# A masked softmax on one core: eight slots in place of twelve, loops in place of unrolled code, the mask bound inside the minimum, the first tile in halves

## The chip, the cores and the metric

One NeuronCore of a Trainium2 chip. The metric is the device time of the kernel in microseconds, the median of several executions. Profiles are of one execution each; their span is about 2 us shorter than the timed figure.

## The reference

For each of 16 batches, the softmax over the first `length` of 256 columns; the rest of the row is zero. The data are fp32, 33.5 MB in and 33.5 MB out.

```python
batch, heads, seq_q, seq_k = 16, 8, 256, 256
lengths = np.random.randint(seq_k // 2, seq_k, size=batch)
for b in range(batch):
    masked = x[b, :, :, :lengths[b]] - max over the last axis
    result[b, :, :, :lengths[b]] = exp(masked) / sum(exp(masked))
```

## The kernel before

One batch is one tile of 128 partitions x 16 rows x 256 columns (2.1 MB). The kernel takes the minimum with a bound that is hugely negative beyond the length (no maximum is subtracted), lets ScalarE compute the exponential with its row sum, and lets VectorE multiply by the reciprocal. SyncE loads batches 0 to 3 whole; GpSimd loads the other 12, cut to the smallest of some fixed widths that holds the length.

```python
slots = min(12, batch); ahead = min(4, batch)
xt = pool.tile([P, slots, nt, seq_k], F32, name="xt")
...                                     # SyncE: four loads, then the stores in pieces
load(nc.sync, 0, seq_k)
for b in range(1, ahead):
    load(nc.sync, b, seq_k)
for b in range(batch):
    for s in parts(b):
        nc.sync.wait_ge(s_out, 2 * b + (s.stop - 1) // half + 1)
        nc.sync.dma_start(out=out_f[b, :, s, :], in_=xt[:, b % slots, s, :]).then_inc(s_st[b], 16)
...                                     # GpSimd: zero fills, then 12 loads, unrolled
nc.gpsimd.wait_ge(s_v, 1)
for b in range(ahead, slots):
    nc.gpsimd.memset(xt[:, b, :, low:], 0.0).then_inc(s_fill, 1)
nc.gpsimd.wait_ge(s_ld[ahead - 2], 16)
for n in range(ahead, batch):
    if n < slots:
        nc.gpsimd.wait_ge(s_fill, n - ahead + 1)
    else:
        nc.gpsimd.wait_ge(s_st[n - slots], 16 * len(parts(n - slots)))
    pick(length(POOL, n), n, widths + [seq_k])
...                                     # VectorE: the bound of a batch, and the minimum with it
nc.vector.tensor_scalar(out=cap[:, b % 4, :], in0=iota_h, scalar1=len_s[:, b : b + 1],
                        scalar2=-1.0e30, op0=ALU.subtract, op1=ALU.mult)
nc.vector.tensor_tensor(out=t, in0=t, in1=cap[...].to_broadcast(...), op=ALU.min)
```

The softmax here doesn't subtract the row's maximum and nothing guards it: scores larger than these inputs give would overflow.

## Time and profile before

| | before |
|---|---|
| time, median of 3 runs | 157.55 us (157.49 to 157.84) |
| span of the profile | 155.7 us |
| bytes moved | 62.11 MB, 399 GB/s over the span |
| VectorE / ScalarE busy | 121.3 us / 105.2 us |

The prediction shows the lines and reads them. Here is how to read them. In the rows of 40 slices a digit is the busy share of one slice in tenths. A line of a group gives source line, engine, operation, output<-inputs, count, then busy us, mean ns of one, then the idle time just before these instructions and what ended it. q0 is the queue of DMAs that GpSimd issues, q1 that of SyncE's. A line of a wait gives who waited, for what, us in total, how many times, and the longest. A queue's ring is its line of transfers that are issued and not yet moved.

```profile
SPq L119 <- DVE xt L221: 117.0, 29, 15.4
```

```profile
2.83 0.15 DVE L171 CAST len_b<-word 1x16 bf16<-1x16 int32 x1
2.97 11.04 POOL L145 MEMSET xt<- 128x1536 f32 x8 [0.27 <-DVE iota_h L169]
...
8.96 2.29 DVE L194 TENSOR_TENSOR xt<-xt,cap 128x2048 f32<-128x2048 f32 x1 [3.00 <-DMA xt<-in_x_dram]
...
18.59 17.98 SPq L119 DMA_DIRECT2D out_dram<-xt  x9
```

The first mask begins at 8.96 us, the first store is issued at 18.59.

### The profile page before, as it was taken

The page shows a single profiled execution, that of the slowest core. Times are in us where ns is not written, and L with a number is a line of the kernel's source. Part 1 is how long each engine was busy: PE and PEld are TensorE (multiplying, and loading weights), DVE is VectorE, ACT ScalarE, POOL GpSimd, SP SyncE. Part 2 cuts the span into 40 slices and gives each one's busy share as a digit, 9 for nine tenths or more (in the row PEclk, how much of TensorE's full clock was granted, in tenths as well). Part 3 has the DMA queues.
Part 4 walks back from the last instruction along what each step waited for, and adds up shares of the span by engine and source line. Part 5 has one row for each costly group of instructions (what it writes and reads, how often), then busy time and mean ns, then how long its engine had stood idle before and what let it go on. Part 6 is the DMA issues. An engine that isn't in the chain of part 4 may idle for free.

```text
span 155.7 us, 1168 instructions
## 1 busy us (share of the span) xinstructions
PE 0.2 (0%) x1; PEld 0.1 (0%) x1; DVE 121.3 (78%) x99; ACT 105.2 (68%) x514; POOL 25.1 (16%) x27
## 2 busy tenths in 40 slices
PE   0000000000000000000000000000000000000000
PEld 0000000000000000000000000000000000000000
DVE  2567999999999998949995999997977999910000
ACT  3009999997979695957978397979592989400000
POOL 5996045743001102010000000000000000000000
DMA  4999999999999999999999999999999999999990
GB/s 131 417 450 417 434 368 388 412 445 415 390 398 409 413 421 408 426 400 411 415 412 419 403 409 412 408 418 409 422 436 416 423 434 427 442 429 438 406 402 25
DMA packets 10311, 62.11 MB, mean 399 GB/s; under 512 B 914, under 2 KB 1010, under 8 KB 7106
## 3 DMA queue, kind: packets, MB, share of 16 engines
q1 hardware_dynamic: 6192, 41.95, 65.4%
q0 software_dynamic: 4112, 20.12, 32.0%
q14 instruction: 5, 0.04, 0.1%
q10 hardware_dynamic: 2, 0.00, 0.0%
HBM read 28.51 MB, written 33.55 MB: 399 GB/s over the span
## 4 chain that ended last, share of the span: by engine, by line
DVE 33%; DMA 30%; issue 12%; POOL 6%; another core or an unknown queue 4%; POOLq 1%; SPq 1%; DVEq 0%
DMA xt<-in_x_dram 30%; DVE xt L221 18%; DVE xt L194 12%; POOL xt L145 4%; POOL xt L108 2%; DVE inv_sum L219 1%; DVE cap L179 1%; POOLq L100 1%; SPq L108 1%; POOLq L133 0%; DVEq L207 0%; POOLq L135 0%; DVEq L206 0%; SPq L269 0%
## 5 line engine op out<-in xcount | busy, mean ns | idle before, releaser
L237 ACT ACTIVATE xt<-xt x256 | 102.4, 401 | 27.2 <-DVE xt L194 27.2
L221 DVE TENSOR_TENSOR xt<-xt,inv_sum 128x2048 f32<-128x2048 f32 x32 | 73.3, 2292 | 1.1
L237 ACT ACTIVATION_READ_ACCUMULATOR xt<-xt x256 | 47.8, 187 | 0.0
L194 DVE TENSOR_TENSOR xt<-xt,cap 128x2048 f32<-128x2048 f32 x16 | 36.6, 2287 | 11.6 <-DMA xt<-in_x_dram 11.5
L108 POOL DMA_DIRECT2D xt<-in_x_dram x12 | 12.8, 1065 | 41.3 <-issue 41.3
L145 POOL MEMSET xt<- 128x1536 f32 x8 | 11.0, 1427 | 0.3 <-DVE iota_h L169 0.3
L179 DVE TENSOR_SCALAR cap<-iota_h,len_s 128x256 f32<-128x256 f32 x16 | 9.1, 572 | 0.0
L219 DVE RECIPROCAL inv_sum<-row_sum 128x8 f32<-128x8 f32 x32 | 6.3, 195 | 0.0
L169 DVE TENSOR_SCALAR iota_h<-iota_i 128x256 f32<-128x256 int32 x1 | 0.3, 294 | 2.6 <-POOL iota_i L139 2.6
L230 ACT ACT_TABLE_LOAD x1 | 1.3, 1283 | 1.5 <-SPq L81 1.5
L138 POOL DMA_DIRECT2D word_p<-in_lengths_dram x1 | 0.6, 633 | 1.1 <-SPq L81 1.1
L173 DVE COPY len_s<-len_f 128x16 f32<-128x16 f32 x1 | 0.2, 176 | 0.3 <-PE len_f L158 0.3
L139 POOL IOTA iota_i<- 128x256 int32 x1 | 0.4, 360 | 0.1
L230 ACT ACTIVATE warm<-const-float32-0.0 128x1 f32<-128x1 f32 x1 | 0.2, 203 | 0.0
L142 POOL MEMSET ones<- 1x128 bf16 x1 | 0.2, 195 | 0.0
L158 PE MATMUL len_f<-len_b,ones 1*128 1x16 bf16 x1 | 0.2, 167 | 3.1 <-DVE len_b L171 3.1
L171 DVE CAST len_b<-word 1x16 bf16<-1x16 int32 x1 | 0.2, 154 | 0.0
L258 POOL MEMSET const-float32-0.0<- 128x1 f32 x1 | 0.1, 99 | 0.2 <-issue 0.2
L158 PEld LDWEIGHTS len_f<-len_b,ones 1*128 1x128 bf16 x1 | 0.1, 100 | 3.1 <-POOL ones L142 3.1
L258 POOL MEMSET const-float32-1.0<- 128x1 f32 x1 | 0.1, 98 | 0.0
L258 POOL MEMSET const-bfloat16-1.0<- 128x1 bf16 x1 | 0.1, 98 | 0.0
L258 POOL MEMSET const-uint8-127<- 128x1 uint8 x1 | 0.1, 98 | 0.0
## 6 DMA issues: line engine op xcount, KB each, us to landing
out_dram<-xt SPq DMA_DIRECT2D x16, 1024.0 KB, 24.0
out_dram<-xt SPq DMA_DIRECT2D x20, 512.0 KB, 24.3
xt<-in_x_dram SPq DMA_DIRECT2D x4, 2048.0 KB, 14.4
out_dram<-xt SPq DMA_DIRECT2D x3, 2048.0 KB, 19.1
xt<-in_x_dram POOLq DMA_DIRECT2D x3, 1728.0 KB, 54.8
xt<-in_x_dram POOLq DMA_DIRECT2D x2, 2048.0 KB, 38.3
xt<-in_x_dram POOLq DMA_DIRECT2D x2, 1600.0 KB, 36.6
xt<-in_x_dram POOLq DMA_DIRECT2D x2, 1280.0 KB, 62.5
```

The lines of the kernel that those rows point to most:

```text
L100: return nc.values_load((word_p if engine == POOL else word)[0:1, 2 * b : 2 * b + 1], engines=[engine], skip_runtime_bounds_check_because= ...
L108: engine.dma_start(out=xt[:, b % slots, :, :w], in_=x_f[b, :, :, :w]).then_inc(s_ld[b], 16)
L138: nc.gpsimd.dma_start(out=word64_p, in_=lengths[None, :]).then_inc(s_word_p, 16)
L139: nc.gpsimd.iota(iota_i, pattern=[[1, seq_k]], base=0, channel_multiplier=0).then_inc(s_iota, 1)
L145: nc.gpsimd.memset(xt[:, b, :, low:], 0.0).then_inc(s_fill, 1)
L179: nc.vector.tensor_scalar(out=cap[:, b % 4, :], in0=iota_h, scalar1=len_s[:, b : b + 1], scalar2=-1.0e30, op0=ALU.subtract, op1=ALU.mult,)
L194: return nc.vector.tensor_tensor(out=t[:, :, lo:hi], in0=t[:, :, lo:hi], in1=cap[:, b % 4, None, lo:hi].to_broadcast([P, nt, hi - lo]), op ...
L219: step(nc.vector.reciprocal(out=inv_sum[:, b, s], in_=row_sum[:, b, s]))
L221: ins = nc.vector.tensor_tensor(out=t[:, s, :], in0=t[:, s, :], in1=inv_sum[:, b, s, None].to_broadcast([P, half, seq_k]), op=ALU.mult,)
L230: nc.scalar.activation(out=warm, in_=nc.const_aps.tensor(0.0, (P, 1), F32), func=EXP)
L237: ins = nc.scalar.activation(out=e, in_=e, func=EXP, accum_out=row_sum[:, bass.ds(i, 1), j],)
L258: nc = _bacc.Bacc("TRN2", target_bir_lowering=False, num_devices=1)
```

## The change

Its intent: shorter programs and less memory at no loss, some work taken off VectorE, and an earlier first store. The core of the diff, cut:

```diff
-    slots = min(12, batch)
+    slots = 8
-        load(nc.sync, 0, seq_k)
+        for h in range(2):
+            s = slice(h * half, (h + 1) * half)
+            nc.sync.dma_start(out=xt[:, 0, s], in_=x_f[0, :, s]).then_inc(s_ld[h], 16)
 ...
+                if b >= 2 and s.start == 0:
+                    nc.sync.wait_ge(s_b, 64 * (b // 2 + 1))      # store b waits for store b-2
 ...
-        for n in range(ahead, batch):
-            ...
-            pick(length(POOL, n), n, widths + [seq_k])
+        with nc.Fori(0, (batch - ahead) // 2, 1, engines=[POOL]) as q:
+            for par in range(2):
+                n = 2 * q + (ahead + par)
+                v_len = length(POOL, word_p[0:1, bass.ds(2 * n, 1)])
+                with nc.gpsimd.If(q >= 1):
+                    nc.gpsimd.wait_ge(s_sw[par], 16 * q)         # load n-2
+                    nc.gpsimd.wait_ge(s_st[par], 64 * q)         # store n-8
+                pick(v_len, bass.ds(n, 1), bass.ds(n % slots, 1), par, widths + [seq_k])
 ...
-            return nc.vector.tensor_tensor(out=t, in0=t, in1=cap, op=ALU.min)
+            return nc.vector.scalar_tensor_tensor(
+                out=t, in0=down, scalar=len_s[:, b : b + 1], in1=t, op0=ALU.add, op1=ALU.min)
 ...
-        mask(0)                       # then mask(b+1) ahead of both divides of b
+        mask(0, slice(0, half))
+        mask(0, slice(half, nt))      # then divide(0, 0), mask(1), divide(0, 1), ...
 ...
-        for first, last in ((0, slots), (slots, batch)):      # ScalarE: 16 rows a round
+        with nc.Fori(0, 2 * batch, 1, engines=[ACT]) as i:    # ScalarE: 8 rows a round
```

GpSimd's iota now comes ahead of its DMA of the lengths.

More of the change, by code (lines that the diff above doesn't have):

```diff
@@ L14 @@
 EXP = mybir.ActivationFunctionType.Exp
-SP = mybir.EngineType.SP
 DVE = mybir.EngineType.DVE
@@ L36 @@
     half = nt // 2
+    quarter = nt // 4
     x_f = x.rearrange("b h q k -> b (h q) k").rearrange("b (p t) k -> b p t k", p=P)
     out_f = out.rearrange("b h q k -> b (h q) k").rearrange("b (p t) k -> b p t k", p=P)
-    slots = min(12, batch)
-    ahead = min(4, batch)
+    slots = 8
+    ahead = 4
+    assert slots - ahead == 4 and batch % slots == 0
     widths = list(range(160, 248, 8))
     low = widths[0]
-    quarter = nt // 4
-    cuts = lambda b: (
-        [0, half, half + quarter, nt]
-        if b < slots - 2
-        else [0, half, nt]
-        if b < slots or b == batch - 1
-        else [0, nt]
-    )
-    def parts(b):
-        return [slice(i, j) for i, j in zip(cuts(b), cuts(b)[1:])]
-    mid = seq_k // 2
+    mid = seq_k // 2
+    big = 1.0e30
+    def parts(b):
+        if b < 10:
+            cuts = [0, half, half + quarter, nt]
+        elif b < 12 or b == batch - 1:
+            cuts = [0, half, nt]
+        else:
+            cuts = [0, nt]
+        return [slice(i, j) for i, j in zip(cuts, cuts[1:])]
     pool = ctx.enter_context(tc.tile_pool(name="all", bufs=1))
@@ L73 @@
     iota_i = pool.tile([P, seq_k], I32, name="iota_i")
-    iota_h = pool.tile([P, seq_k], F32, name="iota_h")
-    cap = pool.tile([P, 4, seq_k], F32, name="cap")
+    down = pool.tile([P, seq_k], F32, name="down")
     row_sum = pool.tile([P, batch, nt], F32, name="row_sum")
@@ L78 @@
     warm = pool.tile([P, 1], F32, name="warm")
-    sem = lambda n: ctx.enter_context(nc.semaphore(n))
+    seed = pool.tile([1, 2], F32, name="seed")
     with tc.tile_critical(no_gpsimd_drain=True):
+        sem = lambda n: ctx.enter_context(nc.semaphore(n))
         s_word = sem("s_word")
@@ L86 @@
         s_lenf = sem("s_lenf")
-        s_ld = [sem(f"s_ld{b}") for b in range(batch)]
-        early = batch - slots
-        s_st = [sem(f"s_st{b}") for b in range(early)] + [sem("s_st")] * slots
+        s_ld = [sem(f"s_ld{k}") for k in range(ahead + 1)]
+        s_sw = [sem("s_sw0"), sem("s_sw1")]
+        s_st = [sem("s_st0"), sem("s_st1")]
         s_iota = sem("s_iota")
@@ L96, with length @@
         s_out = sem("s_out")
-        def length(engine, b):
+        def length(engine, at):
             return nc.values_load(
-                (word_p if engine == POOL else word)[0:1, 2 * b : 2 * b + 1],
+                at,
                 engines=[engine],
@@ L104, in length, with pick @@
             )
-        def load(engine, b, w):
-            engine.dma_start(
-                out=xt[:, b % slots, :, :w], in_=x_f[b, :, :, :w]
-            ).then_inc(s_ld[b], 16)
-        load(nc.sync, 0, seq_k)
+        for h in range(2):
+            s = slice(h * half, (h + 1) * half)
+            nc.sync.dma_start(out=xt[:, 0, s], in_=x_f[0, :, s]).then_inc(s_ld[h], 16)
         nc.scalar.dma_start(out=word64, in_=lengths[None, :]).then_inc(s_word, 16)
         for b in range(1, ahead):
-            load(nc.sync, b, seq_k)
+            nc.sync.dma_start(out=xt[:, b], in_=x_f[b]).then_inc(s_ld[b + 1], 16)
         for b in range(batch):
+            s_b = s_st[b % 2]
             for s in parts(b):
                 nc.sync.wait_ge(s_out, 2 * b + (s.stop - 1) // half + 1)
+                if b >= 2 and s.start == 0:
+                    nc.sync.wait_ge(s_b, 64 * (b // 2 + 1))
                 nc.sync.dma_start(
                     out=out_f[b, :, s, :], in_=xt[:, b % slots, s, :]
-                ).then_inc(s_st[b], 16)
-        nc.sync.wait_ge(s_st[-1], 16 * sum(len(parts(b)) for b in range(early, batch)))
-        def pick(v, b, ws):
+                ).then_inc(s_b, 16 * ((s.stop - s.start) // quarter))
+        for par in range(2):
+            nc.sync.wait_ge(s_st[par], 64 * (batch // 2 + 1))
+        def pick(v, n, slot, par, ws):
             if len(ws) == 1:
-                load(nc.gpsimd, b, ws[0])
+                w = ws[0]
+                nc.gpsimd.dma_start(
+                    out=xt[:, slot, :, :w], in_=x_n[:, n, :, :w]
+                ).then_inc(s_sw[par], 16)
                 return
@@ L133, in pick @@
             with nc.gpsimd.If(v <= ws[m]):
-                pick(v, b, ws[: m + 1])
+                pick(v, n, slot, par, ws[: m + 1])
             with nc.gpsimd.Else():
-                pick(v, b, ws[m + 1 :])
-        nc.gpsimd.dma_start(out=word64_p, in_=lengths[None, :]).then_inc(s_word_p, 16)
+                pick(v, n, slot, par, ws[m + 1 :])
+        x_n = x_f.rearrange("b p t c -> p b t c")
         nc.gpsimd.iota(
@@ L142 @@
         nc.gpsimd.memset(ones, 1.0).then_inc(s_ones, 1)
+        nc.gpsimd.dma_start(out=word64_p, in_=lengths[None, :]).then_inc(s_word_p, 16)
+        for par in range(2):
+            nc.gpsimd.memset(seed[:, par : par + 1], 0.0).then_inc(s_st[par], 64)
         nc.gpsimd.wait_ge(s_v, 1)
@@ L146 @@
         nc.gpsimd.wait_ge(s_word_p, 16)
-        nc.gpsimd.wait_ge(s_ld[ahead - 2], 16)
-        for n in range(ahead, batch):
-            if n < slots:
-                nc.gpsimd.wait_ge(s_fill, n - ahead + 1)
-            else:
-                nc.gpsimd.wait_ge(s_st[n - slots], 16 * len(parts(n - slots)))
-            pick(length(POOL, n), n, widths + [seq_k])
+        nc.gpsimd.wait_ge(s_fill, slots - ahead)
+        nc.gpsimd.wait_ge(s_ld[ahead - 1], 16)
+        with nc.Fori(0, (batch - ahead) // 2, 1, engines=[POOL]) as q:
+            for par in range(2):
+                n = 2 * q + (ahead + par)
[4 more added lines that the diff above has]
+                pick(v_len, bass.ds(n, 1), bass.ds(n % slots, 1), par, widths + [seq_k])
         nc.tensor.wait_ge(s_ones, 1)
@@ L168 @@
         nc.vector.wait_ge(s_iota, 1)
-        step(nc.vector.tensor_scalar(out=iota_h, in0=iota_i, scalar1=0.5, scalar2=None, op0=ALU.add))
+        step(
+            nc.vector.tensor_scalar(
+                out=down, in0=iota_i, scalar1=0.5, scalar2=-big, op0=ALU.add, op1=ALU.mult
+            )
+        )
         nc.vector.wait_ge(s_word, 16)
@@ L172 @@
         nc.vector.wait_ge(s_lenf, 1)
-        step(nc.vector.tensor_copy(out=len_s, in_=len_f))
-        nc.vector.wait_ge(s_v, v)
-        def make_cap(b):
-            step(
-                nc.vector.tensor_scalar(
-                    out=cap[:, b % 4, :],
-                    in0=iota_h,
-                    scalar1=len_s[:, b : b + 1],
-                    scalar2=-1.0e30,
-                    op0=ALU.subtract,
-                    op1=ALU.mult,
-                )
-            )
-            return v
@@ L190 @@
-        cap_at = {b: make_cap(b) for b in range(2)}
-        def clip(b, lo, hi):
-            t = xt[:, b % slots]
-            return nc.vector.tensor_tensor(
-                out=t[:, :, lo:hi],
-                in0=t[:, :, lo:hi],
-                in1=cap[:, b % 4, None, lo:hi].to_broadcast([P, nt, hi - lo]),
-                op=ALU.min,
-            )
-        def mask(b):
-            if b + 1 < batch and b + 1 not in cap_at:
-                cap_at[b + 1] = make_cap(b + 1)
-            v_len = length(DVE, b)
-            nc.vector.wait_ge(s_v, cap_at[b])
-            nc.vector.wait_ge(s_ld[b], 16)
-            with nc.vector.If(v_len < mid):
-                clip(b, 0, mid)
-            clip(b, mid, seq_k).then_inc(s_min, 1)
@@ L211 @@
-        mask(0)
-        for b in range(batch):
-            if b + 1 < batch:
-                mask(b + 1)
-            t = xt[:, b % slots]
-            for h in range(2):
-                s = slice(h * half, (h + 1) * half)
-                nc.vector.wait_ge(s_exp, 2 * b + h + 1)
-                step(nc.vector.reciprocal(out=inv_sum[:, b, s], in_=row_sum[:, b, s]))
-                nc.vector.wait_ge(s_v, v)
-                ins = nc.vector.tensor_tensor(
-                    out=t[:, s, :],
-                    in0=t[:, s, :],
-                    in1=inv_sum[:, b, s, None].to_broadcast([P, half, seq_k]),
-                    op=ALU.mult,
-                )
-                ins.then_inc(s_out, 1)
@@ L230 @@
-        nc.scalar.activation(out=warm, in_=nc.const_aps.tensor(0.0, (P, 1), F32), func=EXP)
-        for first, last in ((0, slots), (slots, batch)):
-            with nc.Fori(first, last, 1, engines=[ACT]) as i:
-                nc.scalar.wait_ge(s_min, i + 1)
-                slot = i - first
-                for j in range(nt):
-                    e = xt[:, bass.ds(slot, 1), j, :]
-                    ins = nc.scalar.activation(
-                        out=e,
-                        in_=e,
-                        func=EXP,
-                        accum_out=row_sum[:, bass.ds(i, 1), j],
-                    )
-                    if (j + 1) % half == 0:
-                        ins.then_inc(s_exp, 1)
+        step(
+            nc.vector.tensor_scalar(
+                out=len_s, in0=len_f, scalar1=big, scalar2=None, op0=ALU.mult
+            )
+        )
@@ new lines, with clip, mask @@
+        nc.vector.wait_ge(s_v, v)
+        def clip(b, s, lo, hi):
+            t = xt[:, b % slots, s, lo:hi]
+            return nc.vector.scalar_tensor_tensor(
+                out=t,
+                in0=down[:, None, lo:hi].to_broadcast([P, s.stop - s.start, hi - lo]),
+                scalar=len_s[:, b : b + 1],
+                in1=t,
+                op0=ALU.add,
+                op1=ALU.min,
+            )
+        def mask(b, s):
+            v_len = length(DVE, word[0:1, 2 * b : 2 * b + 1])
+            if b == 0:
+                nc.vector.wait_ge(s_ld[s.start // half], 16)
+            elif b < ahead:
+                nc.vector.wait_ge(s_ld[b + 1], 16)
+            else:
+                nc.vector.wait_ge(s_sw[b % 2], 16 * ((b - ahead) // 2 + 1))
+            with nc.vector.If(v_len < mid):
+                clip(b, s, 0, mid)
+            clip(b, s, mid, seq_k).then_inc(s_min, (s.stop - s.start) // half)
@@ new lines, in divide @@
+        def divide(b, h):
+            s = slice(h * half, (h + 1) * half)
+            nc.vector.wait_ge(s_exp, 2 * b + h + 1)
+            step(nc.vector.reciprocal(out=inv_sum[:, b, s], in_=row_sum[:, b, s]))
+            nc.vector.wait_ge(s_v, v)
+            t = xt[:, b % slots, s, :]
+            nc.vector.tensor_tensor(
+                out=t,
+                in0=t,
+                in1=inv_sum[:, b, s, None].to_broadcast([P, half, seq_k]),
+                op=ALU.mult,
+            ).then_inc(s_out, 1)
@@ new lines @@
+        mask(0, slice(0, half))
+        mask(0, slice(half, nt))
+        for b in range(batch):
+            if b == 0:
+                divide(0, 0)
+            if b + 1 < batch:
+                mask(b + 1, slice(0, nt))
+            if b > 0:
+                divide(b, 0)
+            divide(b, 1)
+        nc.scalar.activation(out=warm, in_=nc.const_aps.tensor(0.0, (P, 1), F32), func=EXP)
+        x_h = xt.rearrange("p s (h j) c -> p (s h) j c", h=2)
+        sum_h = row_sum.rearrange("p b (h j) -> p (b h) j", h=2)
@@ L247 @@
+        with nc.Fori(0, 2 * batch, 1, engines=[ACT]) as i:
+            nc.scalar.wait_ge(s_min, i + 1)
+            at = bass.ds(i % (2 * slots), 1)
+            for j in range(half):
+                e = x_h[:, at, j, :]
+                ins = nc.scalar.activation(
+                    out=e, in_=e, func=EXP, accum_out=sum_h[:, bass.ds(i, 1), j]
+                )
+            ins.then_inc(s_exp, 1)
 _INS = ['x', 'lengths']
```

## The prediction

> **What bounds the kernel now.** I read the page first, for which row is full; then the busy time by stretch, for where it is full; then the queues of one stretch, for what shares the full resource; then the groups and the timelines, for how close the engines come to being the limit themselves.
>
> The page: span, two rows of the 40 slices (each 3.9 us), and the two DMA queues (packets, MB, share of the 16 engines' span).
>
> ```profile
> span 155.7 us, 1168 instructions
> ...
> DVE  2567999999999998949995999997977999910000
> ...
> DMA  4999999999999999999999999999999999999990
> GB/s 131 417 450 417 434 368 388 412 445 415 390 398 409 413 421 408 426 400 411 415 412 419 403 409 412 408 418 409 422 436 416 423 434 427 442 429 438 406 402 25
> ...
> q1 hardware_dynamic: 6192, 41.95, 65.4%
> q0 software_dynamic: 4112, 20.12, 32.0%
> ```
>
> The DMA row is 9 from the second slice to the last but one. VectorE is at 9 too for long stretches, but its row is 0 for the last four slices, while the DMA stays full: what ends the kernel is transfer, not arithmetic. q0 holds the 12 loads that GpSimd issues (cut to a width of 160 to 256 columns by the batch's length); q1 holds the first four loads and every store.
>
> By stretch (columns: PE, PEld, DVE, ACT, POOL busy us, clock, DMA share, GB/s):
>
> ```profile
> 20.00:30.00 10.00, 0.00 (x0) 0.00 (x0) 9.93 (x9) 10.00 (x51) 6.16 (x6) 1.00 0.99 387
> ...
> 60.00:70.00 10.00, 0.00 (x0) 0.00 (x0) 7.89 (x7) 6.58 (x33) 1.02 (x2) 1.00 1.02 414
> ...
> 110.00:120.00 10.00, 0.00 (x0) 0.00 (x0) 8.06 (x7) 6.49 (x32) 0.00 (x0) 1.00 1.03 432
> ...
> 140.00:150.00 10.00, 0.00 (x0) 0.00 (x0) 0.00 (x0) 0.00 (x0) 0.00 (x0) 1.00 0.99 423
> 150.00:156.00 6.00, 0.00 (x0) 0.00 (x0) 0.00 (x0) 0.00 (x0) 0.00 (x0) 1.00 0.30 128
> ```
>
> After 140 us all compute engines show 0.00 and the DMA still moves 423 GB/s: a backlog of stores is drained. The sum of the bytes confirms it: 62.11 MB in all, less 0.52 MB before 4 us (131 GB/s) and 0.77 MB after 150 us (128 GB/s), is 60.8 MB in 146 us, 417 GB/s. So time = about 2.5 us until the stream starts, 62.11 MB at 417 GB/s = 149 us, some 4 us for the last landing and the end of the span, and about 2 us by which the timed run (157.55) exceeds the span (155.7).
>
> The queues in the stretch from 60 to 90 us:
>
> ```profile
> q1 hardware_dynamic: 1388, 6.62, 54.3%
> q0 software_dynamic: 1393, 5.75, 47.8%
> ```
>
> Both always have work, and take turns. The groups (busy us, mean ns of one, idle before):
>
> ```profile
> L237 ACT ACTIVATE xt<-xt x256 | 102.4, 401 | 27.2 <-DVE xt L194 27.2
> L221 DVE TENSOR_TENSOR xt<-xt,inv_sum 128x2048 f32<-128x2048 f32 x32 | 73.3, 2292 | 1.1
> ...
> L194 DVE TENSOR_TENSOR xt<-xt,cap 128x2048 f32<-128x2048 f32 x16 | 36.6, 2287 | 11.6 <-DMA xt<-in_x_dram 11.5
> ...
> L179 DVE TENSOR_SCALAR cap<-iota_h,len_s 128x256 f32<-128x256 f32 x16 | 9.1, 572 | 0.0
> ```
>
> VectorE waits 11.5 us for loads in its masks, ScalarE 27.2 us for VectorE. From the timelines, three instructions of VectorE and the last four loads of GpSimd:
>
> ```profile
> 21.19 2.29 DVE L194 TENSOR_TENSOR xt<-xt,cap 128x2048 f32<-128x2048 f32 x1
> ...
> 28.55 2.27 DVE L194 TENSOR_TENSOR xt<-xt,cap 128x2048 f32<-128x2048 f32 x1
> ...
> 134.71 2.29 DVE L221 TENSOR_TENSOR xt<-xt,inv_sum 128x2048 f32<-128x2048 f32 x1
> ```
>
> ```profile
> 35.47 1.26 POOL L108 DMA_DIRECT2D xt<-in_x_dram x1 [2.37 <-issue]
> 50.01 1.15 POOL L108 DMA_DIRECT2D xt<-in_x_dram x1 [13.28 <-issue]
> 59.31 1.15 POOL L108 DMA_DIRECT2D xt<-in_x_dram x1 [8.15 <-issue]
> 67.50 0.56 POOL L108 DMA_DIRECT2D xt<-in_x_dram x1 [7.04 <-issue]
> ```
>
> VectorE, when never waiting, takes 28.55 - 21.19 = 7.36 us a batch; the DMA takes 149 / 16 = 9.3 us. VectorE's last work ends at 137.0, some 17 us before the transfers: 17 us at 425 GB/s is 7 MB, over three batches of stores. The four loads reuse the slots of batches 0 to 3, so they tell when those stores had landed: about 34, 49, 58 and 66 us, some 10.7 us apart.
>
> [...]
>
> **The change, part by part.**
> (1) Bytes: none. The widths of the 12 loads are picked as before, and the stores are cut as before (ten batches in three pieces, two in two, three whole, the last in two: 39 both times). The sum of 149 us stays.
> (2) Mask: 16 bounds of 572 ns go, 9.1 us busy, but most of that overlaps: in the steady cadence one adds only about 0.27 us, the 20.93 to 21.19 us between its start and that of the mask behind it. The minimum becomes scalar-tensor-tensor over the same 2048 columns. [...] it costs 2.29 us, and VectorE's cadence is 7.36 - 0.27 = 7.1 us against the DMA's 9.3. Gain on the path: none; it was waiting for loads already.
> (3) First tile in halves: its first half should land about 2.4 us sooner (1 MB at 430 GB/s), and the first store can be issued at some 13.5 us: half landed at 6.5 (mask 0 began at 8.96), half a mask 1.15, eight exponentials 8 x 0.4 = 3.2, divide 2.3, latencies. Before it was 18.6. But the store enters the same ring behind loads 1 to 3 (8.4 MB, done at about 21 us at 430 GB/s), so it starts to move at 21 us either way. What is left is a fuller store queue in the stretch 20 to 30 us, which ran at 387 instead of 411 GB/s: at most 10 x 24 / 411 = 0.6 us, and I count half, 0.3 us.
> (4) ScalarE's loop over halves: 32 rounds in place of 16; 256 exponentials at 0.40 us as before, 6.4 us a batch, perhaps 0.3 us for one more loop turn (the idle 0.31 us that one batch's start shows). Under 7.1 us: nothing on the path.
> (5) Eight slots, and at most two loads and two stores in flight: load n now waits for load n-2 and store n-8, store b for store b-2. Loads landed some 8.4 us apart in the later part (mask 8 waited until 68.8, mask 14 until 117.9). When load n-2 lands, load n-1 still has some 8 us in the ring, and GpSimd needs 2 to 3 us for its branches and its 1.15 us issue: q0 does not run dry. Store n-8, from the 10.7 us spacing: store 0 at 34 against load 6 at about 50 (needed for load 8), store 4 at 77 against load 10 at 85, store 7 at 109 against load 13 at 108. The slack shrinks to nothing for the last load, but load 14 then still covers 8 us. When a store lands, the one behind it holds 2.1 MB, 5 us at full rate, longer than a wake-up. So both rings stay fed, and the round robin stays as it was.
> Sum: 157.55 - 0.3 = 157.2 us.
>
> **The rivals.**
> A: the mask at half rate. [...] I give it one chance in five.
> B: the slots or the short queues starve the DMA. For: the slack of about zero at the last load. Against: VectorE's lead at the end is 17 us. Load 15 landed before 125 us; its mask, exponentials and divides took 12 us, and a last half store 4.5. To reach 161 us it would have to land some 17 us later. I expect 0 to 1.5 us.
> C: fewer loads queued give stores a larger share early, or the fuller store queue helps more: all would have to come from 411 GB/s rising towards 432. Over 100 us of mixed traffic that would be 5 us at most; nothing in the change alters packet sizes, so I count on under 1 us.
>
> **Range and chances.** The main line gives 156.5 to 158 us; B adds up to 1.5[...]. Predicted 157.2, range 155.8 to 160.2. Slower by 2% means over 160.7: most of half of A, and a little of B, 0.11. Faster by 2% means under 154.4, which needs C in full: 0.03. Within: 0.86.
>
> **What would show it.** DMA row still at 9 with about 62.1 MB; q0 and q1 packets equal in mid-run, q0 ending at about 121 us; the mask's group at about 2290 ns for the 15 whole tiles; VectorE ending 10 us or more before the span does. The prediction is wrong if [...] DMA slices in the middle fall below 9.

Passages are cut out of the text above, and the cuts are marked: rules and figures that no trace or run of this case shows. They are the paragraph ahead of the parts of the change, with an upper limit on what another order could win; in part (2) the condition for the 2.29 us, that the new mask runs as fast as the minimum it replaces (2287 ns), which no run had shown yet; and the arithmetic of rival A, the reasons for and against it, and two clauses of the last paragraphs that used it. The sum came to 157.55 - 0.3 = 157.2 us, but its zero for the mask rests on that condition. Rival A's came to 159.5 to 162.5 us; it stands in the range's upper end and in the chance of 0.11. The wake-up of part (5), given there without a figure, is short in the trace after: in 14 waits for a store SyncE issued the next one 0.06 to 0.07 us after the landing.

## More of the kernel before

```profile
20.00:24.00 4.00, 0.00 (x0) 0.00 (x0) 3.96 (x5) 4.00 (x21) 1.78 (x3) 1.00 0.97 363
```

Before, every store waits for VectorE alone, and the little cast of the lengths (2.83 us) comes just ahead of GpSimd's fills (2.97 us).

## The result, and the profile after

| | before | after |
|---|---|---|
| time, median of 6 runs each | 157.61 us (157.44 to 157.84) | 157.14 us (156.85 to 157.49) |
| ratio of fast runs | | 0.997 (95%: 0.9954 to 0.9985) |
| span of the profile | 155.7 us | 155.5 us |
| VectorE busy | 121.3 us | 120.0 us |
| GB/s, 20 to 24 us | 363 | 293 |

A ratio is the mean time of one kernel's fast runs over the mean of the other's of the same rounds, so it is not quite the ratio of the medians. Executions over 1.5% slower than the fastest of the same kernel are left out of the means. The change is within 2%, 0.3% faster and just clear of noise.

The page of the kernel after:

```profile
DVE  4963999999999968939895999997977999920000
...
DMA  4999999999999999999999999999999999999991
GB/s 116 428 443 426 434 312 388 416 442 427 393 395 410 415 416 406 420 410 413 409 412 419 402 417 406 415 411 405 425 421 432 420 419 432 457 426 422 415 434 61
...
q1 hardware_dynamic: 6336, 41.95, 65.9%
q0 software_dynamic: 4112, 20.12, 32.0%
```

The bytes of both queues are those of before. The DMA row is full again from the second slice, and VectorE's row again ends in four zeros. (Single slices of the GB/s row reach 450 before and 457 after because the view books all of a packet's bytes at its start. With the bytes spread over each packet's own time, read from the kept traces, every microsecond from 16 to 20 us has 429 to 432 GB/s in both kernels.) The queues of the stretch from 60 to 90 us, after:

```profile
q1 hardware_dynamic: 1381, 6.59, 54.1%
q0 software_dynamic: 1377, 5.76, 47.9%
```

They still take turns one to one, as before. What did move is who waits for what. The waits of SyncE's queue, after:

```profile
SPq L118 <- DMA out_dram<-xt: 98.5, 14, 11.0
```

SyncE used to wait for VectorE for 117.0 us; now 98.5 us are waits for an earlier store. It looks alarming and costs nothing that shows: while SyncE waits for store b-2, store b-1 is in the ring, and the DMA row stays at 9.

The groups of VectorE after, with different shapes kept apart:

```profile
L197 DVE SCALAR_TENSOR_TENSOR xt<-down,len_s,xt 128x2048 f32<-128x2048 f32 x15 | 35.2, 2347 | 10.2 <-DMA xt<-in_x_dram 10.2
...
L185 DVE CAST len_b<-word 1x16 bf16<-1x16 int32 x1 | 5.6, 5595 | 0.4 <-DMA word<-in_lengths_dram 0.4
```

The new mask takes 2347 ns, against 2287 before: 2.6% more, so no half rate. The second line is the surprise: a cast of 16 numbers takes 5.6 us. The timeline of the first 17 us, after, shows why:

```profile
2.30 5.59 DVE L185 CAST len_b<-word 1x16 bf16<-1x16 int32 x1 [0.40 <-DMA word<-in_lengths_dram]
...
2.54 5.33 POOL L151 MEMSET xt<- 128x1536 f32 x4
...
9.29 2.48 DVE L197 SCALAR_TENSOR_TENSOR xt<-down,len_s,xt 128x1024 f32<-128x1024 f32 x2 [0.87 <-DVE len_s L188]
...
16.73 5.82 SPq L119 DMA_DIRECT2D out_dram<-xt  x3
```

The cast ends at 7.89 us, with the last of the fills at 7.87. The fills now come before the cast has run, and the first mask needs the lengths; so the first half tile, landed by about 6.5 us (as the run with the later fills shows), waits until 9.29 us, later than the whole tile of before (8.96). The cast took 5595 ns, where it took 154 ns before. What holds it can't be read from the stamps alone: the cast's record starts 0.24 us ahead of that of the fills, and at its old length it would have been over before them. That it is the fills that hold it is shown by the run with the later fills, below.

### The profile page after: what moved, and what is told of

Read it like the earlier page. It is cut to its first block, busy times and chain, and to the rows that moved or that the text cites. A ratio compares the mean times of both kernels' runs of the same rounds, so it can differ in the third digit from the quotient of the medians.

```text
span 155.5 us, 1320 instructions
## 1 busy us (share of the span) xinstructions
PE 0.2 (0%) x1; PEld 0.1 (0%) x1; DVE 120.0 (77%) x84; ACT 105.1 (68%) x514; POOL 19.4 (12%) x26
## 3 DMA queue, kind: packets, MB, share of 16 engines
q1 hardware_dynamic: 6336, 41.95, 65.9%
## 4 chain that ended last, share of the span: by engine, by line
DMA 67%; DVE 11%; issue 6%; POOLq 2%; SPq 1%; POOL 0%; DVEq 0%
DMA xt<-in_x_dram 60%; DVE xt L224 7%; DMA out_dram<-xt 7%; DVE xt L197 3%; POOLq L100 1%; POOLq L136 1%; POOLq L131 1%; SPq L109 1%; DVE inv_sum L221 0%; POOL xt L131 0%; SPq L112 0%; POOLq L159 0%; POOLq L155 0%; DVEq L214 0%; POOLq L161 0%
## 5 line engine op out<-in xcount | busy, mean ns | idle before, releaser
L251 ACT ACTIVATE xt<-xt x256 | 102.4, 402 | 27.2 <-DVE xt L197 27.2
L197 DVE SCALAR_TENSOR_TENSOR xt<-down,len_s,xt 128x2048 f32<-128x2048 f32 (+1 forms) x17 | 37.7, 2222 | 11.1 <-DMA xt<-in_x_dram 10.2
L185 DVE CAST len_b<-word 1x16 bf16<-1x16 int32 x1 | 5.6, 5595 | 0.4 <-DMA word<-in_lengths_dram 0.4
L151 POOL MEMSET xt<- 128x1536 f32 x4 | 5.3, 1392 | 0.0
```

The lines of the kernel that those rows point to most:

```text
L185: nc.vector.tensor_copy(out=len_b, in_=word[:, ::2]).then_inc(s_lenb, 1)
L197: return nc.vector.scalar_tensor_tensor(out=t, in0=down[:, None, lo:hi].to_broadcast([P, s.stop - s.start, hi - lo]), scalar=len_s[:, b : ...
L251: ins = nc.scalar.activation(out=e, in_=e, func=EXP, accum_out=sum_h[:, bass.ds(i, 1), j])
```

## The experiments

Theory T: the transfers alone set the time, and every part of the change lies off that path. Rivals: a lighter VectorE, fewer queued loads, or the earlier first store made the 0.3%; the mask has little slack; the slots have little slack. Twelve kernels were run.

**The mask alone.** In the kernel before, the bounds go and the minimum becomes the new form.

```diff
-step(make_cap ...)   # 16 bounds
-nc.vector.tensor_tensor(out=t, in0=t, in1=cap, op=ALU.min)
+nc.vector.scalar_tensor_tensor(out=t, in0=iota_h, scalar=len_s[:, b : b + 1], in1=t, op0=ALU.add, op1=ALU.min)
```

> The kernel before with one part alone: the bound is added inside the minimum, the 16 separate bounds are gone. Theory T (transfers set the end, the mask is off the path): 157.3 to 157.9 us, ratio to before within 0.3% of 1, VectorE cadence about 7.1 in place of 7.36 us, mask about 2350 ns, waits of VectorE for loads longer by what it saves. Rival (the 0.3% came from a lighter VectorE): ratio about 0.997, 157.1 us.

Measured: 157.46 us, ratio 0.9987 (0.9973 to 1.0002). Its groups:

```profile
L178 DVE SCALAR_TENSOR_TENSOR xt<-iota_h,len_s,xt 128x2048 f32<-128x2048 f32 x16 | 37.6, 2349 | 17.5 <-DMA xt<-in_x_dram 17.4
```

VectorE's busy time fell from 121.3 to 114.5 us, by 6.8, and its waits for loads rose from 11.5 to 17.4, by 5.9. What VectorE saves here, off the path, it waits.

**Eight slots alone.** In the kernel before, with the pieces of the stores kept.

```diff
-    slots = min(12, batch)
+    slots = min(8, batch)
```

> The kernel before with eight slots in place of twelve and nothing else (same store pieces). Theory T: 157.3 to 158.0 us, q0 and q1 packets still equal from 60 to 90 us, q0 ending at about 121 us. Rival B (slots starve the transfers): DMA slices under 9 in mid-run and a time over 158.5 us. Rival (fewer loads queued gave the 0.3%): ratio about 0.997.

Measured: 157.34 us, ratio 0.9979 (0.9964 to 0.9994), 1387 packets of q1 to 1388 of q0 from 60 to 90 us. No starving; a gain of 0.2% that just clears noise, between theory T and the rival of fewer queued loads. That rival is not excluded for a part of the 0.3%, though fewer slots still do not gain more, as the next run shows.

**Six slots, and five.** The same edit with 6 and with 5.

> The kernel before with six slots, store pieces as they were. At 9.3 us a batch six slots turn round in 56 us. A batch holds its slot for about 16 us of load, 15 to 20 of compute and 20 to 24 of store, together 51 to 60, so loads begin to run dry; but then stores get the whole rate, so the transfers stay full: 157.3 to 159 us. Rival B (short of slots, the transfers starve): over 160.

Measured: 157.64 us, ratio 0.9992 (0.9968 to 1.0015); one of its four runs was slow (160.71 us) and is not counted.

> The kernel before with five slots, one more than the four first loads: 46 us a turn, under the 51 to 60 that a batch holds its slot with both queues full. Theory: now loads and stores must each move faster than with both queues full, holes appear in the DMA row: 158.5 to 163 us. Rival (the split of the rate adapts without holes): within 0.5% of before.

Measured: 159.32 us, ratio 1.0114 (1.0082 to 1.0145). The page with five slots:

```profile
DVE  2264999999919898079699959996971979999900
...
GB/s 121 421 446 417 446 348 413 413 419 430 435 390 409 393 425 409 424 408 408 382 410 416 414 414 413 411 411 415 422 418 414 415 422 434 409 434 181 409 425 167
```

The mid-run that I expected to show holes has none beyond the dip at 20 us (348), which the kernel before has too (368). Even here the split of the rate adapts: from 33.3 to 39.2 us q0 moves no data, and q1 alone fills the engines (419 and 430 GB/s in the two slices from 31.4 to 39.3 us). The hole is at the end, in the slice with 181 GB/s: the last load is issued at 121.9 us (67.5 with twelve slots, 105.4 with eight, 118.1 with six), VectorE works on until 149 us (its row ends in two zeros, not four), and the backlog of stores that used to cover the last batch's arithmetic is used up. So in the kernel before slots run short between six and five, and it shows as a thinner cushion at the end.

**The mask twice.** In the changed kernel each mask is computed once more into a spare tile; the results are the same, and VectorE pays about what a mask at half rate would cost, one more mask of 2347 ns.

```diff
+            step(clip(b, s, mid, seq_k, out=spare[:, s, :]))
+            nc.vector.wait_ge(s_v, v)
             clip(b, s, mid, seq_k).then_inc(s_min, ...)
```

> The changed kernel with each mask computed once more into a spare tile: the same results, VectorE dearer by 16 x some 2.4 us, which is what a mask at half rate would have cost. If VectorE's slack of 17 us at the end is all there is, 38 us more must show: VectorE full from 9 us on, cadence 7.13 + 2.4 = 9.55 us, 9.3 + 2.4 + 16 x 9.55 = 164.5 us, half a store 4.5 behind it: span 167 to 169, time 168 to 171 us, 7 to 8% slower. If transfers alone decide: still 157.

Measured: 174.24 us, ratio 1.1054 (1.1036 to 1.1073). A second mask of a whole tile takes 2.45 us from its start to that of the next (17.95 to 20.40 us, for one). VectorE's row of the page, and the end of the timeline:

```profile
DVE  5887999999999999999999999999999999999910
```

```profile
159.54 5.24 SPq L120 DMA_DIRECT2D out_dram<-xt  x3
...
162.10 2.29 DVE L227 TENSOR_TENSOR xt<-xt,inv_sum 128x2048 f32<-128x2048 f32 x1
```

VectorE is the bound from start to end and finishes at 164.4 us, as expected (164.5). The time is still 3 us over my range, because the tail behind VectorE is 8.0 us (the span is 172.4) and not 4.5. Batch 14 is stored in one piece, so nothing of it can leave before its second half is divided at 159.5; with batch 15 that is 4.2 MB, 9.8 us at 430 GB/s, from 159.5 on. The long pieces cost nothing that shows behind the backlog of the changed kernel (157.14 us, against 157.04 for the transfers alone, below), and cost here, where VectorE is last.

**The fills later.** In the changed kernel the fills wait until the lengths are scaled.

```diff
-        nc.gpsimd.wait_ge(s_v, 1)
+        nc.gpsimd.wait_ge(s_v, 2)
```

> The changed kernel with GpSimd's four fills held back until the lengths have been scaled (a wait for 2 in place of 1). Theory: the cast of the lengths took 5.6 us because it stood behind the fills; it will take about 0.15 us, the first mask begins at about 6.5 us in place of 9.3, the first store is issued at about 14 in place of 16.7. As the store lies behind loads 1 to 3 in its ring, the time changes by under 0.3 us: 156.8 to 157.3. Rival: the early store is worth its full 2.7 us, 154.5.

Measured: 157.27 us, ratio 0.9977 (0.9958 to 0.9995), so no better than the changed kernel's 0.997 of other rounds. Its timeline:

```profile
2.29 0.16 DVE L185 CAST len_b<-word 1x16 bf16<-1x16 int32 x1 [0.39 <-DMA word<-in_lengths_dram]
...
3.04 5.33 POOL L151 MEMSET xt<- 128x1536 f32 x4 [0.45 <-DVE len_s L188]
6.58 1.28 DVE L197 SCALAR_TENSOR_TENSOR xt<-down,len_s,xt 128x1024 f32<-128x1024 f32 x1 [3.60 <-DMA xt<-in_x_dram]
...
14.01 0.42 SPq L119 DMA_DIRECT2D out_dram<-xt  x1
```

The cast is back to 0.16 us, the first mask comes at 6.58 us and the first store at 14.01, all as expected, and the time does not move. Note too that the mask at 6.58 us runs its 1.28 us beside the fills (3.04 to 8.37 us), as long as the second half's at 9.05 us after them, where the cast could not. So the fills were what held the cast, and the early store is worth nothing that these runs can tell, far from the rival's 2.7 us.

**The transfers alone.** In the changed kernel masks, exponentials and divides go, and a store waits for its load (a wrong result).

```diff
-                nc.sync.wait_ge(s_out, 2 * b + (s.stop - 1) // half + 1)
+                nc.sync.wait_ge(s_ld[...] or s_sw[b % 2], ...)     # the load of batch b
-        ... all of mask, divide and ScalarE's loop
```

> The changed kernel with masks, exponentials and divides taken out; every store waits for its load's landing alone (a wrong result on purpose: the inputs come back). The same 62.1 MB in the same pieces on the same queues. Theory T: the transfers alone take nearly as long, 155 to 157.2 us. Rival (waits of stores and loads for the compute engines cost several us): 152 or less.

Measured: 157.04 us, ratio 0.9956 (0.994 to 0.9972). Against the changed kernel's 157.14 (ratio 0.997, of other rounds), all the arithmetic together costs no more than a few tenths of a microsecond; the intervals overlap. This is the plainest proof that the arithmetic is off the path. The run keeps the order of the transfers and the depth of the queues, so it says nothing of these.

**Fewer bytes.** In the changed kernel every load of GpSimd's takes 160 columns. Its output is wrong, which doesn't matter for the time.

```diff
-                w = ws[0]
+                w = low
```

> The changed kernel with every one of GpSimd's 12 loads cut to 160 columns (a wrong result on purpose where a length is over 160), everything else as it was: 536 columns x 2048 rows x 4 B = 4.39 MB fewer. Theory T: the time falls with the bytes, 4.39 MB at 417 GB/s = 10.5 us[...]: 146 to 149 us. Rival (compute or waits set the end): over 154 us.

(A term that no run shows is cut out of this expectation; the range of 146 to 149 us stands as it was written, with that term.)

Measured: 147.16 us, ratio 0.9335 (0.9321 to 0.9348). 4.39 MB fewer, 10.0 us less: 439 GB/s for the marginal byte. T again: the time follows the bytes.

**The hole at 20 us, 1: loads sooner.** Both kernels lose rate from 20 to 24 us, the changed one more (293 GB/s against 363).

```diff
-        nc.gpsimd.wait_ge(s_ld[ahead - 1], 16)
+        nc.gpsimd.wait_ge(s_ld[ahead - 2], 16)
```

> The changed kernel with GpSimd's loads waiting for batch 1 to land and not for batch 2, some 4.8 us sooner. In both kernels the transfers drop from 20 to 24 us (363 GB/s before, 293 after, against 430 ahead of it), as the first four loads are done and load 4, issued at 20.7, has not started to move. Theory: the hole is 0.55 MB, 1.3 us, and closes: load 4 is issued at about 16, the stretch 20 to 24 us runs at over 400 GB/s, 155.7 to 156.5 us. Rival (the hole's bytes are made up later, or load 3 is delayed as much): 156.9 to 157.4.

Measured: 156.78 us, ratio 0.9949 (0.9937 to 0.9961), between the range of the theory and that of the rival. Load 4 was issued at 15.80 us, but the stretch only rose from 293 to 324 GB/s, under a third of what I expected: my reason for the hole was wrong.

**2: both.** Sooner loads and later fills.

> The changed kernel with the fills held back until the lengths are scaled, and the loads sooner as well. The first store is then issued at about 14 us as with the fills alone, load 4 at about 16. Theory: the sum of the two, 155.5 to 156.3 us, the fastest so far; if the first store's place in the ring behind loads 1 to 3 makes it worthless, the same as the sooner loads alone within 0.2 us.

Measured: 156.67 us, ratio 0.9937 (0.9922 to 0.9952), the lowest median of all, but not the sum: it is within 0.2 us of the sooner loads alone, so the later fills add nothing clear. What the sooner loads gain on the changed kernel (0.9949 against 0.997, of other rounds) is at the edge of noise. In the same rounds the transfers alone, in the changed kernel's order, took 157.04: with all its arithmetic this version is no slower.

**3: the first tile in halves alone,** in the kernel before.

```diff
-        load(nc.sync, 0, seq_k)
+        nc.sync.dma_start(out=xt[:, 0, :half], in_=x_f[0, :, :half]).then_inc(s_ld[0], 16)
+        nc.sync.dma_start(out=xt[:, 0, half:], in_=x_f[0, :, half:]).then_inc(s_first, 16)
         # mask 0, its exponentials and divide(0, 0) by halves, ahead of mask 1
```

> The kernel before with one part alone: the first tile is loaded and masked in halves, its first divide comes before mask 1. Here the lengths are cast ahead of the fills, so nothing holds the first mask: it begins at about 6.5 to 7 us, unless the two bounds ahead of it are held up by the fills to a later time (they took 2.4 us in the kernel before, until 5.9). First store at about 14 us in place of 18.6. Theory (the store lies behind loads 1 to 3 in its ring): 157.3 to 157.8 us. Rival (an early store is worth its 4.6 us): 153.

Measured: 158.08 us, ratio 1.0024 (1.0007 to 1.0041): above my range and a little slower than before, just clear of noise, though the first mask came at 6.43 us and the first store at 13.71, just as the prediction had them for the changed kernel.

**4: loads at once,** with no wait for an earlier load, and the later fills.

```diff
-        nc.gpsimd.wait_ge(s_ld[ahead - 1], 16)
```

> The changed kernel with the fills held back and GpSimd's loads waiting for no earlier load at all: load 4 is issued at about 10 us and moves from about 14. What is open: the hole at 20 to 24 us stayed with the loads sooner (322 in place of 293 GB/s) and was there too with no compute at all (262), where stores had been queued since 6.4 us. If it is the start of q0, it moves to about 14 us; if it is the turn of q1 from loads to stores, it stays where q1 turns, somewhat later than 20 us as loads 2 and 3 now share the rate, and is shallower, as q0 is then in full flow. Time 156.0 to 156.7 us.

Measured: 156.95 us, ratio 0.995 (0.9934 to 0.9967), a little above my range.

The rate by stretch shows what the hole goes with (columns as in the prediction, the last is GB/s). The changed kernel, the first tile in halves alone, the transfers alone (its ScalarE is idle and has no column), and the loads at once:

```profile
16.00:20.00 4.00, 0.00 (x0) 0.00 (x0) 3.97 (x4) 2.12 (x12) 0.00 (x0) 1.00 1.01 430
20.00:24.00 4.00, 0.00 (x0) 0.00 (x0) 3.97 (x4) 4.00 (x22) 1.71 (x2) 1.00 0.96 293
```

```profile
20.00:24.00 4.00, 0.00 (x0) 0.00 (x0) 3.93 (x5) 4.00 (x22) 1.69 (x2) 1.00 0.93 287
```

```profile
20.00:24.00 4.00, 0.00 (x0) 0.00 (x0) 0.00 (x0) 1.74 (x2) 1.00 0.93 262
```

```profile
20.00:24.00 4.00, 0.00 (x0) 0.00 (x0) 3.65 (x3) 4.00 (x21) 0.00 (x0) 1.00 1.03 409
24.00:26.00 2.00, 0.00 (x0) 0.00 (x0) 1.97 (x3) 2.00 (x11) 0.00 (x0) 1.00 0.89 269
```

With the transfers alone, stores had been issued behind the loads from 6.4 us on, and the hole is deepest: it is no lack of work. With the loads at once q0 moves from about 15 us, and no hole comes there; it moves to 24 to 26 us, where q1 runs out of loads and turns to stores, as loads 2 and 3 now share the rate. So the hole goes with q1's turn from loads to stores.

Packet by packet, the kept traces say more. In the changed kernel the 16 KB packets of SyncE's last loads that start between 21 and 22 us take 1.14 us in the median, where those from 12 to 20 us take 0.61; the first packet of a store starts only at 23.43. (Before: 0.79 us, and 22.67.) So it is the last packets of the loads that slow down, while stores stand behind them. Why is open.

What makes it deeper is open too. All eight kernels with the first tile in halves that turn near 20 us have 262 to 324 GB/s from 20 to 24 us, all five with a whole first tile 350 to 371. The count of stores that stand ready does not explain it by itself: the mask twice issues its first store at 18.05 us, half a microsecond ahead of the kernel before, and has 311; the later fills issue theirs 2.7 us ahead of the changed kernel and have 299 against 293. These rates are of one execution each. Against 430 GB/s, 371 to 262 over 4 us is a loss of 0.6 to 1.6 us (an estimate from these rates).

## Why the prediction was right

The predicted time was 157.2 us, in a range of 155.8 to 160.2; 157.14 was measured. By its own steps:

1. *The bytes stay, and they set the time.* Right. The transfers alone take 157.04 us, and 4.39 MB fewer take 10.0 us off.
2. *The mask as fast as the minimum it replaces: no gain on the path.* Right: 2347 ns against 2287, a cadence of 35.60 - 28.46 = 7.14 us where 7.1 stood, and alone 0.9987. But the 572 ns of a bound was a misleading mean: beside the fills two bounds took 2.41 us together and a third 1.53, where later ones take 0.35. The kernel before thus showed already what short instructions of VectorE can take beside the fills (though not all do: the copy of the lengths, at 3.33 us, took 0.18).
3. *The first tile in halves: first mask at 6.5, first store at 13.5, a gain of 0.3 us from a fuller store queue.* This step failed, twice. In the changed kernel the mask came at 9.29 us and the store at 16.73, as the fills held the cast that I had left out. And the gain did not come, if anything it has the wrong sign: with the fills out of the way the time did not move, in the kernel before the halves alone gave 1.0024, and the stretch I meant to fill, 20 to 30 us, fell from 387 to 364 GB/s. That the store would lie uselessly behind loads 1 to 3 was right (those are 6.3 MB; the 8.4 MB written there are loads 0 to 3).
4. *ScalarE's loop: nothing.* Its busy time stayed (105.1 us), as did its waits for VectorE (27.2 us). The loop was not run alone.
5. *Eight slots and short queues keep both rings fed.* Right: packets one to one, q0 ended at about 123 us in both kernels (I had read 121), and load 15, issued at 109.67 us, landed at about 123.7, in time for its mask at 124.89 (before: 124.97). The margin was thinner than I gave. I counted 2 to 3 us for GpSimd's branches and issue and left out the way from issue to first packet: 4.2 to 5.3 us in the ten cases read where q0 was empty (from 19.98 to 25.27 us in the kernel before, 20.71 to 25.71 in the changed one, 15.80 to 20.30 with the loads sooner, 10.57 to 15.03 with the loads at once); in these four the issue's own record takes 1.20. In the run with the loads sooner q0 moved no data from 37.7 to 38.7 us for that reason. The loads' spacing was 8.2 us ((117.9 - 68.8) / 6) and not 8.4, which changes nothing.

The sum, 157.55 - 0.3, thus hit the 157.14 by luck, with a wrong term. The 0.3% that was measured did not come from the halves. Alone, the slots gave 0.9979, the mask 0.9987, the halves 1.0024; together 0.999, against 0.997 for the whole. The difference is within the intervals, and ScalarE's loop, GpSimd's loop and the short queues were not run alone, so where the last 0.2% comes from stays open.

*Rival A* (a mask at half rate) did not happen, but its size was wrong. The doubled mask costs 2.45 us each and gave 174.2. Half rate taken as twice the plain minimum's 2287 ns adds 2.29 us instead, 16 x 0.16 = 2.6 us less, and another 2.7 for a first mask at 6.58 us in place of 9.29 makes about 169 (an estimate from these measured times), where I wrote 159.5 to 162.5: 3.5 us of the miss is the tail of 8.0 us behind VectorE, which I took for 4.5. That is clear of the 160.7 us that I took for the limit, so all of A and not "most of half of A" would have been slower by 2%, and the chance of being slower by 2%, which I put at 0.11, should have been about 0.2. *Rival B* (slots) begins between six slots and five, in the kernel before; fewer slots with the short queues were not run. *Rival C* was small, as said, though its reason was not quite right: the first tile in halves does change packets, 6336 in q1 where 6192 were, 128 of 16 KB fewer.

## What to carry to other kernels

Before weighing a change on engines, take the arithmetic out and time the transfers alone: if that gives the same time, no change of arithmetic can help. It does not bound what another order of the transfers may give, since it keeps the one it has. What is left there shows in the GB/s row, not in the DMA row: that reads 9 in the slice with 312 GB/s. A shift of work at the start can put a tiny instruction behind a long one on another engine (here 5595 ns in place of 154): look at the mean of each group for one that is absurdly long for its size. When the compute engines do become the bound, the size of the last stores counts, which a backlog had hidden (a tail of 8.0 us with the mask twice).
